# A two-layer token mixer on one NeuronCore: new numbers for the build-time order of its instructions, and the squares of two token tiles put behind the first tile's scaling

## The chip, the cores and the metric

The kernel runs on one core of one Trainium2 chip. The metric is the device time of one launch in microseconds (us). An execution under the profiler also gives a trace: every instruction of TensorE (PE), its weight loads (PEld), VectorE (DVE), ScalarE (ACT), GpSimd (POOL) and SyncE (SP, which issues most transfers), with start and end.

## What is computed

One inference step through two layers, for 128 context tokens and 256 latent tokens of width 1024, three tiles of 128 tokens in all. The context tokens have their own modulation and read only themselves; the latent tokens also read cached keys, values and recurrent states.

```python
def trunk_layer(x, mod, p, lb_f, lb_b, rope, ctx_k, ctx_v, s0_f, s0_b):
    sh1, sc1, g1, sh2, sc2, g2 = jnp.split(mod, 6, axis=-1)
    h = rmsnorm(x, p['norm1_g']) * (1 + sc1) + sh1
    proj = h @ p['w_in']
    q_r, f_f, f_b, i_r, g_r, q_a, k_a, v_a = jnp.split(proj, ...)
    ...
    o_f, s_f = gla_chunked(qr, -jnp.expm1(lf_f), vr, lf_f, s0_f)
    o_b, s_b = gla_chunked(qr[:, ::-1], -jnp.expm1(lf_b)[:, ::-1], vr[:, ::-1], lf_b[:, ::-1], s0_b)
    o_r = rmsnorm(o_f + o_b[:, ::-1], p['hgrn_norm_g']).reshape(B, T, W_R) * jax.nn.silu(g_r)
    ...
    o_a = attend_blocks(qa, k_all, v_all)
    x = x + g1 * (jnp.concatenate([o_r, o_a], axis=-1) @ p['w_out'])
    h2 = rmsnorm(x, p['norm2_g']) * (1 + sc2) + sh2
    x = x + g2 * (jnp.square(jax.nn.relu(h2 @ p['w1'])) @ p['w2'])
    return x, ka, va, s_f, s_b
```

`mod` is `silu(c) @ w_mod + b_mod`, `gla_chunked` a gated linear recurrence run in both directions (4 heads of 128), `attend_blocks` a softmax attention with 8 query and 2 key heads of 64. A last rmsnorm ends both outputs.

## The kernel before

Every large product is made in three passes: a weight is split into a rounded high part (`hi`, a cast on ACT, L413) and the rest (`lo`, a subtraction on DVE, L421), the activations likewise (`Hh`, `Hl`; `mAh`, `mAl`), and TensorE adds hi·Hh, hi·Hl and lo·Hh. These are the **dense** steps: w_in by tokens (L615), by features (L669) and for queries and keys (L639, L640), w_out (L703), w1 (L1218, L1233) and w2 (L1244), 256 to 512 columns a step.

Between them stand TensorE's small groups. In the kernel's words their kinds are "m": modulation products (L457, L468), the levels of the recurrence (L1012, L1026) and the products of attention with V (L927); "t": transposes (L479, L557, L762, L821, L822, L881, L916, L1095, L1148, L1283); "f": scores of attention (L859, L897) and the recurrence's states and outputs (L1101, L1124, L1127, L1128). Several work on a half or a quarter of the array (64 or 32 rows or columns).

No engine's program is written out by hand. Each piece of work is a generator that yields steps `S(engine, duration, function, reads, writes, buffers acquired, buffers released, kind, hold)`. At build time the planner `Sched` (L42 to L148) plays them against a simple clock with estimated durations, and emits, over and over, the step that can go first. Three things weigh in its choice. `start_of` adds `hold` to a small PE step's time when TensorE is in a dense stretch (L100), so that the step lets dense steps pass until others of its sort are ready; between two small groups only `min(hold, SLACK)` counts. `SWITCH` is the cost that the planner believes a change of kind has. And the number given to `spawn` ranks chains when several could go at once. HOLD_M stands at modulation products and their transposes and at L762, HOLD_A in attention, HOLD_Q at the transposes of queries and keys, HOLD_O at the recurrence's states and outputs, HOLD_L at its levels.

At the start, three token tiles `x_92`, `x_93`, `x_94` arrive by DMA. For each, `rms_steps` squares one half on ACT and one on DVE (L533), adds (L539), raises to the power −1/2 on POOL (L541), and `norm_half` scales (L552) and transposes (L557). In the recurrence's output, ACT squares the heads, DVE forms the mean squares (L522), POOL the power (L524), DVE scales with the gate (L1143), TensorE transposes (L1148), and ACT and DVE split the result into `Hh` and `Hl` (L1153) for w_out.

Of the kernel before, what the change touches and what calls it, by code (L numbers as in the profile page):

```python
# [19 lines left out]
SMC = 480  # L20
LAG = HEAD + 1
HOLD_L = 1.0
HOLD_M = 2.0
HOLD_A = 1.0
HOLD_O = 1.0
HOLD_Q = 1.0
BX_T = 0
QN = 3
QG = 2
SLACK = 0.5  # L30
FG_P = 3.0
AP_ACT = ((1, 0),)
HFM = (1,)
# [7 lines left out]
class Sched:  # L41
# [3 lines left out]
    LAT = {"PE": 0.2, "DVE": 0.19, "ACT": 0.13, "POOL": 0.15, "SP": 0.1}  # L45
    OWN = {"PE": 0.0, "DVE": 0.06, "ACT": 0.14, "POOL": 0.1, "SP": 0.0}

    SWITCH = {("d", "m"): 0.11, ("d", "f"): 0.1, ("d", "t"): 0.02, ("m", "d"): 0.2, ("f", "d"): 0.1, ("t", "d"): 0.09,
              ("m", "t"): 0.09, ("m", "f"): 0.05, ("f", "m"): 0.09, ("f", "t"): 0.05, ("t", "m"): 0.09, ("t", "f"): 0.01}
    DMA0, DMA1 = 1.3, 1.8  # L50
    DMAE = 0.7
# [116 lines left out]
def step_kernel(tc, A):  # L168
    nc = tc.nc
    sch = Sched()  # L170
# [34 lines left out]
    x = [sb(f"x{t}", [128, 1024]) for t in range(NT)]  # L205
# [166 lines left out]
    def split_prio():  # L372

        left = sum(1 for k in sch.bound if k[0] == "lo")
        return 0.5 if left <= 1 else 6

    def rcls(u):
        return "raw0" if u in early else "raw"
# [46 lines left out]
    def mod_acc(l, tag):  # L425
        us = mod_units(l, tag)
        acc = {(i, h): ("modacc", l, tag, i, h) for i in range(2) for h in range(2)}
        for u in us:
            for i in range(2):
                for h in range(2):  # L430
                    def f(u=u, i=i, h=h):
                        raw = get(("raw",) + u)[:, h * 512:(h + 1) * 512]
                        o, c = get(acc[i, h]), cT[:, u[3], i:i + 1]
                        if u is us[0]:
                            V.tensor_scalar(out=o, in0=raw, scalar1=c, scalar2=None, op0=ALU.mult)
                        else:
                            V.scalar_tensor_tensor(out=o, in0=raw, scalar=c, in1=o, op0=ALU.mult, op1=ALU.add)  # L437
                    yield S("DVE", c_dve(512, u is us[0], 1), f, r=[("rawk",) + u, "cT"], acq=([("t2", acc[i, h])] + ([("mtok", ("mtok", l, tag))] if (i, h) == (0, 0) else [])) if u is us[0] else [],
                            rel=[("raw",) + u] if (i, h) == (1, 1) else [], w=[("modacck", l, tag, i, h)] if u is us[-1] else [], key=u)

    def mod_chain(l, tag):
# [29 lines left out]
        if tag[0] == "n":  # L471
# [5 lines left out]
            def tr():  # L477
                for s_ in range(ns):
                    PE.transpose(get(nm2)[:, s_ * 128:s_ * 128 + rw], get(ev)[0:rw, s_ * 128:(s_ + 1) * 128], ident[0:rw, 0:rw])  # L479
            yield S("PE", 0.11 * ns, tr, kind="t", hold=HOLD_M if l or tag[:2] != ("n", 0) else 0.0, r=[nm + (1,), "ident"], acq=[("ps", nm2)], rel=[ev], w=[nm + (2,)])  # L480
            jn = J // 2
# [44 lines left out]
    def rms_steps(nm, t, xi, ss):  # L526

        ps = parts(xi, t)
        for n, (c0, c1) in enumerate(ps):
            j = nm + ("j", n)  # L530
            if (xi, n) == (0, 1) or n == 2:

                yield S("DVE", c_dve(c1 - c0, False, 1), lambda: V.scalar_tensor_tensor(out=get(j)[:, 0:c1 - c0], in0=x[t][:, c0:c1], scalar=1.0, in1=x[t][:, c0:c1], op0=ALU.mult, op1=ALU.mult, accum_out=ss[:, n:n + 1]),  # L533
                        r=[("x", xi, t, c0)], acq=[("t2", j)], rel=[j], w=[nm + ("ss", n)])
            else:
                yield S("ACT", c_act(c1 - c0, False, 1), lambda: ACT.activation(out=get(j).bitcast(BF16)[:, 0:c1 - c0], in_=x[t][:, c0:c1], func=AF.Square, accum_out=ss[:, n:n + 1]),
                        r=[("x", xi, t, c0)], acq=[("t2", j)], rel=[j], w=[nm + ("ss", n)])
            if n:
                yield S("DVE", 0.13, lambda: V.tensor_scalar(out=ss[:, 0:1], in0=ss[:, 0:1], scalar1=ss[:, n:n + 1], scalar2=D * EPS if n == 1 else None, op0=ALU.add, **({"op1": ALU.add} if n == 1 else {})),  # L539
                        r=[nm + ("ss", n - 1), nm + ("ss", n)], w=[nm + ("ms",)] if n == len(ps) - 1 else [])  # L540
        yield S("POOL", 0.46, lambda: PO.tensor_tensor(out=ss[:, 0:1], in0=ss[:, 0:1], in1=pw[:, 0:1], op=ALU.pow), r=[nm + ("ms",), "ini"], w=[nm + ("rs",)])  # L541
# [306 lines left out]
    def att_pair(l, t, g):  # L848
# [29 lines left out]
        def tr():  # L878
            for kv in range(2):
                for j in range(3):  # L880
                    PE.transpose(get(pt[kv])[:, j * 128:(j + 1) * 128], get(pp[kv])[:, j * 128:(j + 1) * 128], ident)  # L881
        yield S("PE", 0.66, tr, kind="t", hold=HOLD_A, r=[nm + (3,)], acq=[("ps", pt[0]), ("ps", pt[1])], rel=pp, w=[nm + (4,)])

# [505 lines left out]
    with tc.manual_schedule():  # L1389
        sch.spawn(start_chain(), 0)  # L1390
        sch.spawn(early_reg(), 0)
        sch.spawn(warm_chain("warm", ["ini"], ("h", 0, 0, 0, 0), 21), 99)
        sch.spawn(const_chain(), 4)
        sch.spawn(load_chain(), 5)
        sch.spawn(hi_chain(), split_prio)
        sch.spawn(lo_chain(), split_prio)
        for l in range(L):
            sch.spawn(brow_chain(l), 4)
            for tag in mod_tags(l)[0] + mod_tags(l)[1]:
                if (l, tag) in mod_dve:  # L1400
                    sch.spawn(mod_acc(l, tag), 5.25)
                sch.spawn(mod_chain(l, tag), 0.1 if (l, tag[:2]) == (0, ("n", 0)) else 1 if (l, tag) in mod_dve else 3)
            if l == 0:
                sch.spawn(start_norm(), 0.2)
            for t in range(NT):
                for g in norm_chain(l, 0, t, 2 * l, lambda: Hh, lambda: Hl, [("wo_pe_done", l - 1)] if l else []):
                    sch.spawn(g, 2 + 0.3 * t * 0.6 if l else 1 + 0.1 * t)
            sch.spawn(rope_prep(l), 3)
            sch.spawn(ck_chain(l), 3)
            for t in range(NT):  # L1410
                sch.spawn(qk_chain(l, t), 2.6)
            sch.spawn(attn_region(l), 1)
            for t in range(NT):
                sch.spawn(att_open(l, t), 1)
            for kv in range(2):
                sch.spawn(att_head_ctx(l, kv), 3.0)
            sch.spawn(att_pv(l, 0), 2)
            for t in (1, 2):
                for g in range(4):
                    sch.spawn(att_pair(l, t, g), 3)  # L1420
                sch.spawn(att_pv(l, t), 2)
            for hp in range(2):
                sch.spawn(hg_reg(l, hp), 1)
                for h2 in range(2):
# [88 lines left out]
```

## Time and profile before

| | us |
|---|---|
| median of three runs | 980.83 (980.47 to 981.52) |
| the profiled execution | 980.09 |
| its span, first to last instruction | 978.3 |
| TensorE busy | 967.2 |
| DVE busy | 686.6 |
| ACT busy | 500.1 |

Busy time is the union of an engine's instructions. Matmuls overlap in the trace: the next starts before the last one has ended, so what a dense step costs is the distance from one start to the next, not its length. The span is 1.8 us shorter than the execution's own time.

### The profile page before, as it was taken

The page shows a single profiled execution, that of the slowest core. Times are in us where ns is not written, and L with a number is a line of the kernel's source. Part 1 is how long each engine was busy: PE and PEld are TensorE (multiplying, and loading weights), DVE is VectorE, ACT ScalarE, POOL GpSimd, SP SyncE. Part 2 cuts the span into 40 slices and gives each one's busy share as a digit, 9 for nine tenths or more (in the row PEclk, how much of TensorE's full clock was granted, in tenths as well). Part 3 has the DMA queues.
Part 4 walks back from the last instruction along what each step waited for, and adds up shares of the span by engine and source line. Part 5 has one row for each costly group of instructions (what it writes and reads, how often), then busy time and mean ns, then how long its engine had stood idle before and what let it go on. Part 6 is the DMA issues. An engine that isn't in the chain of part 4 may idle for free.

```text
span 978.3 us, 17379 instructions
## 1 busy us (share of the span) xinstructions
PE 967.2 (99%) x6936; PEld 836.8 (86%) x6936; DVE 686.6 (70%) x1187; ACT 500.1 (51%) x913; POOL 34.5 (4%) x37
## 2 busy tenths in 40 slices
PE   8999999999999999999999999999999999999997
PEld 5796788889989889889888988888899999999896
DVE  4687687777787989989585969977765444444436
ACT  4566656555543444444454676645664444444332
POOL 0020000100000000000001000001100000000000
PEclk9999999999999999999999999999999999999999
DMA  9967676343677887877534322334246444454511
GB/s 313 306 180 237 220 244 178 88 151 94 193 242 241 255 255 234 245 249 236 174 102 126 102 65 88 114 94 141 86 140 209 147 124 144 145 152 148 193 44 64
DMA packets 140656, 165.39 MB, mean 169 GB/s; under 512 B 5872, under 2 KB 105616, under 8 KB 140064
## 3 DMA queue, kind: packets, MB, share of 16 engines
q1 hardware_dynamic: 140144, 163.50, 54.2%
q8 instruction: 54, 0.88, 0.4%
q10 hardware_dynamic: 432, 0.79, 0.2%
q14 instruction: 26, 0.21, 0.1%
HBM read 161.35 MB, written 2.92 MB: 168 GB/s over the span
## 4 chain that ended last, share of the span: by engine, by line
PE 93%; DMA 3%; DVE 1%; issue 1%; ACT 1%; POOL 1%; SPq 0%; POOLq 0%; ACTq 0%; DVEq 0%
PE bank L1244 26%; PE bank L1218 26%; PE bank L669 11%; PE bank L615 7%; PE bank L703 6%; PE bank L639 3%; PE bank L468 2%; PE bank L1026 2%; PE bank L640 1%; PE bank L927 1%; PE bank L881 1%; PE bank L859 1%; DMA eB<-w_mod_d 1%; PE bank L557 1%; DMA raw<-w_in_d 1%
## 5 line engine op out<-in xcount | busy, mean ns | idle before, releaser
L421 DVE TENSOR_TENSOR lo<-raw,hi 128x1024 fp32r<-128x1024 f32 (+1 forms) x149 | 176.9, 1198 | 51.7 <-ACT hi L413 49.9
L413 ACT CAST hi<-raw 128x1024 fp32r<-128x1024 f32 (+1 forms) x149 | 152.8, 1033 | 103.5 <-DMA raw<-w_d 45.3
L437 DVE SCALAR_TENSOR_TENSOR t<-raw,cT,t 128x512 f32<-128x512 f32 x196 | 135.2, 747 | 8.2 <-DMA raw<-w_mod_d 8.0
L1218 PE MATMUL bank<-mA,hi 128*128 128x384 f32 (+1 forms) x336 | 111.5, 332 | 0.0
L1218 PE MATMUL bank<-mA,lo 128*128 128x384 f32 (+1 forms) x336 | 111.1, 331 | 0.0
L1218 PE MATMUL bank<-mB,hi 128*128 128x384 f32 (+1 forms) x336 | 110.9, 330 | 0.0
L1206 DVE TENSOR_TENSOR mB<-t,mA 128x384 fp32r<-128x384 f32 x64 | 35.7, 558 | 102.9 <-ACT mA L1205 102.9
L1203 ACT ACTIVATE t<-bank 128x384 f32<-128x384 f32 x64 | 31.4, 491 | 140.4 <-PE bank L1218 140.4
L1244 PE MATMUL bank<-lo,mA 128*128 128x512 f32 (+1 forms) x255 | 99.3, 389 | 0.0
L1244 PE MATMUL bank<-hi,mB 128*128 128x512 f32 (+1 forms) x255 | 99.2, 389 | 0.0
L1244 PE MATMUL bank<-hi,mA 128*128 128x512 f32 (+1 forms) x255 | 99.0, 388 | 0.0
L1218 PE MATMUL bank<-mA,wts 128*128 128x384 f32 (+1 forms) x352 | 89.4, 327 | 0.0
L1244 PE MATMUL bank<-wts,mA 128*128 128x512 f32 (+1 forms) x268 | 87.8, 389 | 0.0
L413 ACT CAST wts<-raw 128x1024 fp32r<-128x1024 f32 x44 | 46.1, 1050 | 46.4 <-DMA raw<-w_d 23.4
L421 DVE TENSOR_TENSOR wts<-raw,wts 128x1024 fp32r<-128x1024 f32 x44 | 53.7, 1223 | 21.6 <-ACT wts L413 21.3
L669 PE MATMUL bank<-Hh,hi 128*128 128x384 f32 x192 | 67.8, 353 | 0.0
L1218 PEld LDWEIGHTS bank<-mA,hi 128*128 128x128 f32 x336 | 63.2, 188 | 1.9 <-issue 0.4
L669 PE MATMUL bank<-Hh,lo 128*128 128x384 f32 x192 | 64.5, 336 | 0.0
L1218 PEld LDWEIGHTS bank<-mB,hi 128*128 128x128 f32 x336 | 63.2, 188 | 1.4
L669 PE MATMUL bank<-Hl,hi 128*128 128x384 f32 x192 | 64.4, 335 | 0.0
L1218 PEld LDWEIGHTS bank<-mA,wts 128*128 128x128 f32 x352 | 62.6, 188 | 1.7 <-issue 0.9
L1218 PEld LDWEIGHTS bank<-mA,lo 128*128 128x128 f32 x336 | 63.2, 188 | 0.0
(272 smaller groups left out, 1951.1 us busy)
## 6 DMA issues: line engine op xcount, KB each, us to landing
raw<-w_d SPq DMA_DIRECT2D x128, 512.0 KB, 4.2
raw<-w_mod_d SPq DMA_DIRECT2D x80, 512.0 KB, 3.7
raw<-w_in_d SPq DMA_DIRECT2D x40, 512.0 KB, 5.2
raw<-w_in_d SPq DMA_DIRECT2D x16, 384.0 KB, 5.3
G<-grow SPq DMA_DIRECT2D x4, 1024.0 KB, 6.8
raw<-w_out_d SPq DMA_DIRECT2D x16, 256.0 KB, 4.5
raw<-w_out_d SPq DMA_DIRECT2D x8, 512.0 KB
eB<-w_mod_d SPq DMA_DIRECT2D x12, 256.0 KB, 5.4
```

The lines of the kernel that those rows point to most:

```text
L413: yield S("ACT", c_act(n), lambda u=u, n=n: ACT.copy(out=get(("hi",) + u)[:, 0:n], in_=get(("raw",) + u)[:, 0:n]), r=[("rawk",) + u] + aft ...
L421: yield S("DVE", c_dve(n), lambda u=u, n=n: V.tensor_tensor(out=get(("lo",) + u)[:, 0:n], in0=get(("raw",) + u)[:, 0:n], in1=get(("hi",) + ...
L437: V.scalar_tensor_tensor(out=o, in0=raw, scalar=c, in1=o, op0=ALU.mult, op1=ALU.add)
L468: PE.matmul(get(nm)[32 * j:32 * j + m, 0:N], cT[:, k, 0:m], raw[:, o:o + N], start=k == 0, stop=k == 7, tile_position=(0, 32 * j))
L615: PE.matmul(ps, a, b, start=(first and k == 0 and i == 0), stop=(last and k == kk - 1 and i == 2))
L639: PE.matmul(get(aq), a, b[:, 0:512], start=st and i == 0, stop=sp and i == 2)
L669: PE.matmul(ps, a, b, start=(k == 0 and i == 0), stop=(k == 7 and i == 2))
L703: PE.matmul(ps, a, b, start=j == 0 and i == 0, stop=j == 7 and i == 2)
L1203: yield S("ACT", c_act(384, True), lambda: ACT.activation(out=get(r_)[:, 0:384], in_=get(z)[:, 0:384], func=AF.Relu), r=[z], acq=[("t2", r ...
L1206: yield S("DVE", c_dve(384), lambda: V.tensor_tensor(out=get(u)[1], in0=get(t_)[:, 0:384], in1=get(u)[0].bitcast(F32), op=ALU.subtract), r ...
L1218: PE.matmul(get(z)[:, cs], a, b, start=(k == 0 and i == 0), stop=(k == 7 and i == 2))
L1244: PE.matmul(get(bank)[:, c0 % 512:c0 % 512 + c1 - c0], a, b, start=(f == f0 and i == 0), stop=(f == fl and i == 2))
```

## The change

Five of the holds, `SLACK` and three entries of `SWITCH` get other values; the ranks get names, and of those three get other values: the recurrence's levels (3.5 to 3.0), its states (3 to 3.5) and the activation of the MLP (2 to 3.0). In `rms_steps` the squares on DVE of tiles 1 and 2 in the first norm (`xi == 0 and t`) now also depend on the second half of tile 0's scaling. No step is added or taken away by hand; one more warm-up matmul (L315) results.

```diff
-HOLD_M = 2.0
-HOLD_A = 1.0
-HOLD_O = 1.0
-HOLD_Q = 1.0
+HOLD_M = 3.0
+HOLD_A = 3.0
+HOLD_O = 1.5
+HOLD_Q = 2.0
...
-SLACK = 0.5
+P_LV = 3.0
+P_ST = 3.5
+P_ACTV = 3.0
...
+SLACK = 0.3
...
-    SWITCH = {("d", "m"): 0.11, ("d", "f"): 0.1, ("d", "t"): 0.02, ("m", "d"): 0.2, ("f", "d"): 0.1, ("t", "d"): 0.09,
+    SWITCH = {("d", "m"): 0.11, ("d", "f"): 0.1, ("d", "t"): 0.02, ("m", "d"): 0.25, ("f", "d"): 0.2, ("t", "d"): 0.12,
...
-                        r=[("x", xi, t, c0)], acq=[("t2", j)], rel=[j], w=[nm + ("ss", n)])
+                        r=[("x", xi, t, c0)] + ([("nrm", 0, 0, 0, "xn", 1)] if xi == 0 and t else []), acq=[("t2", j)], rel=[j], w=[nm + ("ss", n)])
...
-                sch.spawn(hg_levels(l, hp), 3.5)
+                sch.spawn(hg_levels(l, hp), P_LV)
...
-                    sch.spawn(hg_state(l, 2 * hp + h2), 3)
+                    sch.spawn(hg_state(l, 2 * hp + h2), P_ST)
...
-            sch.spawn(mlp_act(l), 2)
+            sch.spawn(mlp_act(l), P_ACTV)
```

Where the change shows in the order: in the changed file the lines behind the constants stand 13 higher (L533 is L546 there). Numbers behind names tell buffers apart.

DVE at the start, before: squares (L533), sums (L539) and scalings (L552) of the three tiles `x_92` to `x_94`.

```order
L533 SCALAR_TENSOR_TENSOR t_1_108,sm<-x_92 128x512
L539 TENSOR_SCALAR sm<-sm 128x1
L533 SCALAR_TENSOR_TENSOR t_3_110,sm<-x_93 128x512
L552 TENSOR_SCALAR t_4_111<-x_92,sm 128x512
L552 TENSOR_SCALAR t_5_112<-x_92,sm 128x512
```

The same place after the change (squares L546, sums L552, scalings L565):

```order
L546 SCALAR_TENSOR_TENSOR t_1_108,sm<-x_92 128x512
L552 TENSOR_SCALAR sm<-sm 128x1
L565 TENSOR_SCALAR t_3_110<-x_92,sm 128x512
L565 TENSOR_SCALAR t_4_111<-x_92,sm 128x512
L546 SCALAR_TENSOR_TENSOR t_5_112,sm<-x_93 128x512
L546 SCALAR_TENSOR_TENSOR t_7_114,sm<-x_94 128x512
```

Both scalings of `x_92` moved ahead of the squares of `x_93` and `x_94`.

DVE at the end of layer 1's recurrence, before: mean squares (L522), the scaling of two heads of a tile (L1143), their low parts (L1153) and splits of weights (L421) between them.

```order
L1153 TENSOR_TENSOR Hl<-bank_68,Hh 128x2x128
L522 TENSOR_SCALAR sm<-sm 128x2
L421 TENSOR_TENSOR Hl<-raw_115,Hh 128x1024
L1143 SCALAR_TENSOR_TENSOR t_3_110<-bank_63,sm,tok_4628 128x128 x2
L421 TENSOR_TENSOR mA_6273<-raw_117,mA_6273 128x1024
L421 TENSOR_TENSOR lo_124<-raw_118,hi_120 128x1024
L1153 TENSOR_TENSOR Hl<-bank_63,Hh 128x2x128
L522 TENSOR_SCALAR sm<-sm 128x2
L421 TENSOR_TENSOR lo_125<-raw_116,hi_121 128x1024
L1143 SCALAR_TENSOR_TENSOR t_0_107<-bank_68,sm,tok_4628 128x128 x2
```

The same place after (L535, L1156, L1166 and L434 are those four lines):

```order
L434 TENSOR_TENSOR mA_6280<-raw_115,mA_6280 128x1024
L535 TENSOR_SCALAR sm<-sm 128x2
L1156 SCALAR_TENSOR_TENSOR t_7_114<-bank_64,sm,tok_4629 128x128 x2
L535 TENSOR_SCALAR sm<-sm 128x2
L434 TENSOR_TENSOR lo_124<-raw_116,hi_120 128x1024
L1156 SCALAR_TENSOR_TENSOR t_3_110<-bank_65,sm,tok_4629 128x128 x2
L434 TENSOR_TENSOR lo_125<-raw_117,hi_121 128x1024
L1166 TENSOR_TENSOR Hl<-bank_64,Hh 128x2x128
```

The first tile's scaling (`t_7_114`) now follows its mean square with no split between, and the first low part stands behind the second tile's scaling and both splits.

TensorE at the same place after (L1161 transposes scaled heads, L716 is w_out, L1137 to L1141 the outputs):

```order
L1161 MATMUL bank_64<-cst,t_7_114 128x128 x2
L716 MATMUL bank_63<-mA_6280,Hh 128x512
L716 MATMUL bank_63<-mA_6280,Hl 128x512
...
L1137 MATMUL bank_65<-tok_4629,hg_4834 128x128
L1140 MATMUL bank_65<-hg_4834 128x128
L1141 MATMUL bank_65<-S_103,hg_4834 128x128
...
L1161 MATMUL bank_64<-cst,t_3_110 128x128 x2
L716 MATMUL bank_66<-hi_120,Hh 128x512
L716 MATMUL bank_66<-hi_120,Hl 128x512
```

Before, 25 rows of w_out, the six outputs and the transposes of the next tile lay between the first tile's transposes and the step that reads `hi_120` with `Hl`; now four rows of w_out do, beside those outputs and transposes.

TensorE in layer 1, before: products with V (L927) and two groups of level products of the recurrence (L1026), each between dense steps by features (L669).

```order
L669 MATMUL bank_67<-Hh,lo_123 128x384
L927 MATMUL bank_68<-hg_4839,vS_102 64x512 x2
L927 MATMUL bank_68<-hg_4839,vS_100 64x512 x2
L927 MATMUL bank_68<-hg_4839,vS_101 64x512 x2
L669 MATMUL bank_67<-Hh,hi_119 128x384
...
L669 MATMUL bank_64<-Hh,lo_124 128x384
L1026 MATMUL bank_66<-hg_4838,ones 32x32 x24
L669 MATMUL bank_64<-Hh,hi_120 128x384
...
L1026 MATMUL bank_61<-hg_4838 32x32 x24
```

The same work after (L940 the products with V, L1039 the levels, L682 the dense steps):

```order
L682 MATMUL bank_67<-Hh,lo_125 128x384
L1039 MATMUL bank_61<-hg_4833,ones 32x32 x24
L940 MATMUL bank_68<-hg_4834,vS_102 64x512 x2
L940 MATMUL bank_68<-hg_4834,vS_100 64x512 x2
L940 MATMUL bank_68<-hg_4834,vS_101 64x512 x2
L1039 MATMUL bank_62<-hg_4833 32x32 x24
L682 MATMUL bank_67<-Hh,hi_121 128x384
```

Three excursions from the dense steps have become one.

More of the change, by code (lines that the diff above doesn't have):

```diff
@@ L29 @@
 QG = 2
-SLACK = 0.5
+P_EV = 5.062
+P_MA = 5.25
+P_LV = 3.0
+P_ST = 3.5
+P_HO = 3.6
+P_QK = 2.6
+P_AP = 3.0
+P_AC = 3.0
+P_IG = 1.0
+P_SG = 1.5
+P_ACTV = 3.0
+P_SP = 6.0
+LEFT = 1
+SLACK = 0.3
 FG_P = 3.0
@@ L374, in split_prio @@
         left = sum(1 for k in sch.bound if k[0] == "lo")
-        return 0.5 if left <= 1 else 6
+        return 0.5 if left <= LEFT else P_SP
     def rcls(u):
@@ L1400, in step_kernel @@
                 if (l, tag) in mod_dve:
-                    sch.spawn(mod_acc(l, tag), 5.25)
+                    sch.spawn(mod_acc(l, tag), P_MA)
                 sch.spawn(mod_chain(l, tag), 0.1 if (l, tag[:2]) == (0, ("n", 0)) else 1 if (l, tag) in mod_dve else 3)
@@ L1410, in step_kernel @@
             for t in range(NT):
-                sch.spawn(qk_chain(l, t), 2.6)
+                sch.spawn(qk_chain(l, t), P_QK)
             sch.spawn(attn_region(l), 1)
@@ L1415, in step_kernel @@
             for kv in range(2):
-                sch.spawn(att_head_ctx(l, kv), 3.0)
+                sch.spawn(att_head_ctx(l, kv), P_AC)
             sch.spawn(att_pv(l, 0), 2)
@@ L1419, in step_kernel @@
                 for g in range(4):
-                    sch.spawn(att_pair(l, t, g), 3)
+                    sch.spawn(att_pair(l, t, g), P_AP)
                 sch.spawn(att_pv(l, t), 2)
@@ L1424, in step_kernel @@
                 for h2 in range(2):
-                    sch.spawn(hg_ev(l, hp, h2), 5.062)
-                    sch.spawn(hg_sig(l, hp, h2), 1.5)
-                sch.spawn(hg_levels(l, hp), 3.5)
+                    sch.spawn(hg_ev(l, hp, h2), P_EV)
+                    sch.spawn(hg_sig(l, hp, h2), P_SG)
+                sch.spawn(hg_levels(l, hp), P_LV)
                 for h2 in range(2):
-                    sch.spawn(hg_state(l, 2 * hp + h2), 3)
+                    sch.spawn(hg_state(l, 2 * hp + h2), P_ST)
                 for t in range(NT):
-                    sch.spawn(hg_out(l, hp, t), 3.6)
+                    sch.spawn(hg_out(l, hp, t), P_HO)
                 sch.spawn(hg_fin(l, hp), 3)
             for t in range(NT):
-                sch.spawn(ig_chain(l, t), 1.0)
+                sch.spawn(ig_chain(l, t), P_IG)
                 sch.spawn(xupd_chain(l, "wo", t, 0), 0.03 + 0.3 * t * 0.6)
```

## The prediction

> **What bounds the kernel now.** I read the page first, then TensorE's waits, then its timeline row by row.
>
> ```profile
> span 978.3 us, 17379 instructions
> PE 967.2 (99%) x6936; PEld 836.8 (86%) x6936; DVE 686.6 (70%) x1187; ACT 500.1 (51%) x913; POOL 34.5 (4%) x37
> PEclk9999999999999999999999999999999999999999
> PE 93%; DMA 3%; DVE 1%; issue 1%; ACT 1%; POOL 1%; SPq 0%; POOLq 0%; ACTq 0%; DVEq 0%
> PE bank L315 <- DVE sel L264: 2.1, 1, 2.1
> PE bank L479 <- ACT t L475: 0.9, 2, 0.5
> PE bank L557 <- DVE t L552: 0.6, 1, 0.6
> PE bank L1148 <- DVE t L1143: 0.5, 1, 0.5
> ```
>
> TensorE is busy for 99% of the span, the clock granted is full in every slice, and the chain that ends last is 93% TensorE. Its waits, with the longest ones shown, come to some 4 us, half of that ahead of its first matmul. The next engine, DVE, is busy for 70%. So no other engine can pay unless it makes TensorE wait or stops doing so, and the time is TensorE's own stream: dense matmuls, whose number does not change, small groups put between them, what it costs to leave and re-enter the dense stream, and a few waits.
>
> **The change, part by part.** Counted from the two orders of instructions, TensorE does the same matmuls but for one more warm-up matmul (L315). What moves is their grouping: excursions out of the dense stream fall from 105 to 91, changes of kind from 262 to 233. The question is what an excursion costs beside its own matmuls. Columns of the timeline: start, time from start to end, engine, line, result and operands, shape, number.
>
> ```profile
> 80.58 0.34 PE L669 MATMUL bank<-Hh,lo 128*128 128x384 f32 x1
> 80.75 0.81 PE L881 MATMUL bank<-cst,tok 128*128 128x128 f32 x6
> 81.58 0.34 PE L669 MATMUL bank<-Hl,hi 128*128 128x384 f32 x1
> ...
> 581.20 0.34 PE L669 MATMUL bank<-Hh,lo 128*128 128x384 f32 x1
> 581.38 1.47 PE L881 MATMUL bank<-cst,tok 128*128 128x128 f32 x12
> 582.86 0.34 PE L669 MATMUL bank<-Hl,hi 128*128 128x384 f32 x1
> ```
>
> *Transposes.* Between the two L669 rows of each piece lie the transposes and one more dense step (its row is left out). A 384-column step takes 0.17 from start to start (80.58 to 80.75), so six transposes cost 81.58 − 80.58 less two dense steps of 0.17 = 0.66, and twelve 582.86 − 581.20 − 0.34 = 1.32: 0.11 each, both times, and nothing for the excursion itself. **Fusing two groups of transposes saves nothing.**
>
> ```profile
> 157.69 0.39 PE L615 MATMUL bank<-hi,Hl 128*128 128x512 f32 x1
> 157.92 0.39 PE L615 MATMUL bank<-lo,Hh 128*128 128x512 f32 x1
> 158.23 0.63 PE L1026 MATMUL bank<-hg 128*32 128x32 f32 x48
> 158.79 0.50 PE L615 MATMUL bank<-hi,Hh 128*128 128x512 f32 x1
> 159.13 0.40 PE L615 MATMUL bank<-hi,Hl 128*128 128x512 f32 x1
> ...
> 620.12 0.39 PE L615 MATMUL bank<-lo,Hh 128*128 128x512 f32 x1
> 620.44 1.15 PE L1026 MATMUL bank<-hg 128*32 128x32 f32 x96
> 621.51 0.50 PE L615 MATMUL bank<-hi,Hh 128*128 128x512 f32 x1
> 621.85 0.39 PE L615 MATMUL bank<-hi,Hl 128*128 128x512 f32 x1
> ```
>
> *Groups on a quarter or half of the array* (level products L1026, and with them mod products L468, scores L859, products with V L927). A dense 512-column step takes 0.23 (157.69 to 157.92). The group starts 0.31 after the last dense one (157.92 to 158.23): 0.08 of entry. The first dense step behind it takes 0.34 (158.79 to 159.13): 0.11 of return. One excursion of 48 costs 159.13 − 157.92 − 0.46 = 0.75, one of 96 costs 621.85 − 620.12 − 0.46 = 1.27, so two fused save 0.23. I count, behind the first 45 us, 4 entries and 9 returns to dense fewer (returns fall more because some of these groups now lead into transposes): 4 × 0.08 + 9 × 0.11 = **−1.3**. The ends: 12 excursions fewer at the whole 0.19 give −2.3; if a return is merely deferred through the transposes, 4 × 0.19 = −0.8.
>
> The Trainium skill, in "TensorEngine Tiling (Array Packing)", section Key Properties, says "Mode switching requires drain: Changing tiling mode (not just tile) drains the TensorE". That speaks against the change, since transposes and dense steps share one mode. By the orders changes of shape fall only from 146 to 140; by the rule that is six drains, at an estimate of 0.19 each −1.1. The transposes above, without a constant of their own, agree with it.
>
> *The start.*
>
> ```profile
> 6.22 0.69 DVE L533 SCALAR_TENSOR_TENSOR t<-x 128x512 f32<-128x512 f32 x1 [0.25 <-DMA x<-x_sample_d]
> 6.83 0.88 DVE L552 TENSOR_SCALAR t<-x,sm 128x512 f32<-128x512 f32 x2
> 6.04 0.55 POOL L541 TENSOR_TENSOR sm<-sm,pw 128x1 f32<-128x1 f32 x1 [5.60 <-DVE sm L539]
> 24.78 0.83 ACT L413 CAST hi<-raw 128x768 fp32r<-128x768 f32 x1 [4.74 <-DMA raw<-w_in_d]
> 25.84 0.33 PE L479 MATMUL bank<-cst,t 128*128 128x128 f32 x1 [0.51 <-ACT t L475]
> 33.36 0.33 PE L479 MATMUL bank<-cst,t 128*128 128x128 f32 x1 [0.39 <-ACT t L475]
> ```
>
> Tile 0's scaling (6.83) waits for tile 1's square (6.22 + 0.69 = 6.91), though POOL had its factor at 6.59; the new dependency puts it some 0.2 earlier. The squares of tiles 1 and 2, of 0.69 each, come behind it, and tile 1's scaling about 1 us later. None of it reaches the end: at 24.78 ACT's cast waited for a DMA, and TensorE at 25.84 is behind that same transfer. SP's order, which issues it, is the same there. If this cover were gone, tile 1's delay would cost its 1 us. Behind that gate the new order fuses two groups of mod products (one entry and return, 0.19) and puts a dense step over the wait at 33.36 (0.39), and leaves one dense step of about 0.35 on the late side: −0.19 − 0.39 + 0.35, and the odd warm-up matmul lies ahead of the gate; **−0.3**, within ±0.5.
>
> *The last part of layer 1's recurrence.*
>
> ```profile
> 673.10 0.44 PE L1148 MATMUL bank<-cst,t 128*128 128x128 f32 x2
> 678.10 0.44 PE L1148 MATMUL bank<-cst,t 128*128 128x128 f32 x2 [0.47 <-DVE t L1143]
> 681.36 0.39 PE L703 MATMUL bank<-hi,Hl 128*128 128x512 f32 x1
> 670.80 1.60 POOL L524 TENSOR_TENSOR sm<-sm,pw 128x2 f32<-128x2 f32 x1 [25.34 <-DVE sm L522]
> 675.87 1.53 POOL L524 TENSOR_TENSOR sm<-sm,pw 128x2 f32<-128x2 f32 x1 [3.47 <-DVE sm L522]
> 678.58 0.70 POOL L524 TENSOR_TENSOR sm<-sm,pw 128x2 f32<-128x2 f32 x1 [1.18 <-DVE sm L522]
> 675.63 1.22 DVE L421 TENSOR_TENSOR lo<-raw,hi 128x1024 fp32r<-128x1024 f32 x1
> 677.43 0.61 DVE L1143 SCALAR_TENSOR_TENSOR t<-bank,sm,tok 128x128 f32<-128x128 f32 x2 [0.59 <-POOL sm L524]
> ```
>
> POOL's power takes 0.70 alone and 1.5 to 1.6 when a split of 1.22 runs on DVE beside it; the scaled heads (L1143) and the transposes (L1148) come behind. Three such transposes waited 0.2, 0.26 and 0.64 here by the gaps in their rows, **1.1 in all**. In the new order the scaling of the first tile stands directly behind its mean square, with no split between, and all three transposes stand at least 0.7 us of TensorE work behind what they need: −1.1. But w_out's first step that reads the low part of the first tile's heads (L703 `hi,Hl`) came 8.3 us behind their transposes (673.10 to 681.36), and now it stands one dense step behind the second tile's transposes; on DVE one split (1.22, `lo_125` in the order of the section on the change) stands between the second tile's scaling and the low part that it reads (`Hl<-bank_64`). Scaled heads finish 0.7 ahead of those transposes, so the split ends at 0.5 behind their start; 0.4 for the difference itself and 0.2 to be seen make 1.1, against about 0.6 until that step (two transposes 0.22, one dense step 0.34): a **new wait of 0.5**. Sum **−0.6**. Ends: −1.1 without it; another split or a power of 1.6 in the way, +1.0.
>
> *Attention.* With scores held for three dense steps' time rather than one, score groups, transposes and products with V of a tile stand closer together, so the softmax between them has less cover. Five places have under 1 us of slack by the orders. I take one miss of 0.3 among them: **+0.3**, ends 0 (all covered, as now) and +1.2 (one split of 1.22 ahead). The last twentieth of the program, with the final norm, is in the same order: nothing. ACT and POOL keep the number of their instructions, and DVE's splits are the same 149.
>
> **Sum:** −1.3 − 0.3 − 0.6 + 0.3 = −1.9. The profiled run took 980.09 (span 978.3, 1.8 around it), so 978.2 by it; it lies 0.74 below the median of the three runs, 980.83, so **978.9** on the median's scale.
>
> **Rivals.**
> - *A, every excursion pays.* If every change of kind costs, transposes included, what a group on a part of the array pays by the rows (0.08 in, 0.11 out, and up to 0.1 more of drain in its last matmuls), the 14 excursions fewer at 0.29 are −4: 976.8. The cheaper return of larger groups speaks for it; the transposes at a flat 0.11 against it.
> - *B, given back.* The holds move excursions later, and what consumed them early then waits; each of the five tight places in attention in both layers loses 0.15 and the recurrence's waits return: −1.9 + 1.5 = −0.4, 980.4. For it: TensorE waits for nearly nothing now because its orders were loose. Against: DVE is idle for 30% of the span.
> - *C, slower: w_out waits for the mixed heads of layer 1.* Low parts come behind DVE's splits, in order. With a power at 1.6 rather than 0.7 and two splits rather than one ahead of the low part, the wait named above is 0.5 + 0.9 + 1.22 = 2.6 rather than 0.5, and layer 0 has the same chain: −1.9 + 2.1 + 2.6 = +2.8, 983.6. It decides from the point where the chain behind the transposes takes more than the 0.6 us of cover. For it: the 1.53 power at 675.87; against: in the new order the splits stand behind, not ahead of, the first scaling.
> - *It doesn't do what it says:* the square's new dependency has no effect on TensorE, as costed above; that is part of the forecast.
>
> **How the numbers follow.** The forecast, 977.9 to 979.9 (its largest unknown, the fusing, runs from −2.3 to −0.8), has 0.52; A 0.14; B 0.24; C 0.10. A measurement of this kernel can tell about 0.2%, 1.96 us, from no change, that is 978.87 and 982.79. The forecast sits on the lower one, so half of it counts as faster: 0.26 + 0.14 = 0.40; no change 0.26 + 0.24 = 0.50; slower 0.10. The range leaves out C and the far half of A: 976.8 to 981.5.
>
> **What would show it.** Right: the three waits of L1148 gone, transposes still at 0.11 each whatever the size of their group, two level groups with the product with V between them costing one entry and one return, a wait of about 0.5 at w_out's first low part, TensorE's first dense step behind the DMA at the same time within 0.1. Wrong: the dense step behind transposes becoming longer or shorter (A), new rows in TensorE's waits from DVE on scores or transposes of attention (B), a wait over 1 us at w_out (C). What I can't see in the trace of before is how DVE's queue stands at each of these places: that would be what makes it wrong.

## The result, and the profile after

| | before | after |
|---|---|---|
| median, us | 980.74 (980.47 to 981.52, 4 runs) | 986.83 (985.82 to 987.49, 4 runs) |
| profiled execution, us | 980.09 | 986.21 |
| its span, us | 978.3 | 984.4 |

The changed kernel takes 1.0054 times as long, with an interval of 1.0042 to 1.0066: it is 6.1 us slower, where 1.9 us faster was forecast. The page of the changed kernel, its first lines:

```profile
span 984.4 us, 17384 instructions
PE 968.5 (98%) x6935; PEld 837.9 (85%) x6937; DVE 685.7 (70%) x1187; ACT 499.4 (51%) x913; POOL 41.3 (4%) x37
PEclk9999999999999999999999999999999999999999
```

The profiled execution of e1 below (1188.15, at a granted clock of 0.75) was a slow one and gives no row by place; all other times here are of fast ones. The clock is the same and the engines do the same work, but for one figure: POOL is busy for 41.3 us rather than 34.5 with the same 37 instructions. TensorE's waits after (total, number, longest), without those in the first 10 us and those under 0.4:

```profile
PE bank L835 <- DVE t L820: 1.1, 1, 1.1
PE bank L834 <- DVE t L828: 1.0, 2, 0.8
PE bank L481 <- DMA raw<-w_mod_d: 0.9, 1, 0.9
PE bank L1161 <- DVE t L1156: 0.8, 1, 0.8
PE bank L716 <- DVE t L1156: 0.7, 1, 0.7
PE bank L1137 <- ACT t L1123: 0.6, 1, 0.6
```

Only one of these pairs stood in the list of before, the transposes of scaled heads (L1161 is L1148 there: 0.5, at 678.10 in layer 1); after, its wait stands in layer 0. To see where they fall, I weighed each TensorE instruction of the two traces with the same standard time for its shape and noted when each kernel had done the same amount. The table shows, for stretches named by the time in the kernel before, how much later (or earlier, negative) the other kernel left a stretch than it entered it; the experiments below have their rows in it too. Each row is from one execution, so that a few tenths of a microsecond say little.

| us, against before | 0–36 start | 36–72 queries, keys | 72–192 attention, w_in | 192–210 recurrence outputs | 210–269 w_out, w1 | 269–534 MLP | 534–659 layer 1 attention | 659–701 layer 1 outputs | rest | all |
|---|---|---|---|---|---|---|---|---|---|---|
| after | 0.9 | **2.7** | 0.9 | **3.1** | −0.2 | 0.4 | −1.6 | −0.6 | 0.4 | 6.2 |
| e2 holds | 0.7 | −0.8 | −0.4 | 0.2 | 4.1 | 0.5 | −1.5 | −1.5 | 0.5 | 1.8 |
| e3 after, quiet | 0.7 | −0.1 | 1.3 | 1.1 | 3.5 | 0.1 | −0.3 | 3.9 | 0.0 | 10.3 |
| e4 before, quiet | 0.3 | −0.1 | 1.0 | 0.0 | 3.6 | 0.0 | 0.0 | −1.2 | 0.0 | 3.5 |
| e5 after, heads | −0.1 | 0.1 | 0.6 | 1.1 | −0.2 | 0.4 | −0.3 | 4.1 | 0.1 | 5.8 |
| e6 before, heads | 0.3 | −0.1 | 0.8 | 0.0 | −0.2 | 0.4 | 0.0 | −1.1 | 0.0 | 0.0 |
| e7 after, old switch | 0.0 | −0.8 | −0.6 | 1.4 | −0.2 | 0.4 | −1.4 | 3.5 | 0.0 | 2.4 |
| e8 after, old holds | 0.9 | 1.3 | 2.2 | 0.0 | −0.2 | 0.4 | 0.4 | −0.3 | 0.0 | 4.7 |
| e9 holds, layer 1 | 1.3 | −0.1 | 0.1 | 0.0 | −0.2 | 0.3 | −1.4 | −1.5 | 0.5 | −1.1 |
| e10 holds, split | 0.5 | −0.8 | 0.5 | 0.0 | −0.3 | 0.5 | −1.4 | −1.5 | 0.5 | −2.1 |
| e11 after, no power | 1.0 | 0.6 | 0.4 | 1.7 | −0.3 | 0.4 | −1.6 | −0.7 | 0.4 | 2.1 |
| e12 repaired | 1.3 | −0.8 | 1.6 | 0.0 | −0.3 | 0.1 | −1.4 | 5.1 | 0.0 | 5.7 |

So two places of layer 0 lose 5.8 us, and layer 1 gains 2.2. The waits in the list explain 2.1 of the 2.7 (L835, L834) and 2.1 of the 3.1 (L1161, L716, L1137); what is left is in no wait that the profile lists. The first place, in the changed kernel: DVE and POOL at the mean squares of queries and keys (L535 mean squares, L434 splits, L537 the power, L798 the scaling), and the transpose of a key that waits (L835).

```profile
59.58 0.38 DVE L535 TENSOR_SCALAR sm<-sm 128x8 f32<-128x8 f32 x4
59.86 2.36 DVE L434 TENSOR_TENSOR lo<-raw,hi 128x1024 fp32r<-128x1024 f32 x2
64.07 0.29 DVE L798 TENSOR_TENSOR t<-bank,sm 128x128 f32<-128x128 f32 x1 [1.85 <-POOL sm L537]
59.89 6.06 POOL L537 TENSOR_TENSOR sm<-sm,pw 128x10 f32<-128x10 f32 x2 [1.95 <-DVE sm L535]
65.81 0.33 PE L835 MATMUL bank<-cst,t 128*128 128x128 f32 x1 [1.09 <-DVE t L820]
```

POOL's power begins 0.03 after two splits have begun on DVE. Two such powers take 6.06, where before two took 3.89:

```profile
54.10 3.89 POOL L524 TENSOR_TENSOR sm<-sm,pw 128x10 f32<-128x10 f32 x2 [44.69 <-DVE sm L522]
```

The second of the pair in the changed kernel has no split beside it and takes its 1.95; the first takes 4.1, and it ends 1.8 after the splits' end at 62.22, which is nearly a whole power. **The power did not run slowly beside the splits: it stood until they had ended.** DVE then had nothing to do for 1.85, and TensorE waited for the key. The second place, layer 0's recurrence outputs, DVE and POOL in the changed kernel:

```profile
203.19 0.17 DVE L535 TENSOR_SCALAR sm<-sm 128x2 f32<-128x2 f32 x1
203.27 1.22 DVE L434 TENSOR_TENSOR lo<-raw,hi 128x1024 fp32r<-128x1024 f32 x1
205.08 0.61 DVE L1156 SCALAR_TENSOR_TENSOR t<-bank,sm,tok 128x128 f32<-128x128 f32 x2 [0.59 <-POOL sm L537]
203.44 1.61 POOL L537 TENSOR_TENSOR sm<-sm,pw 128x2 f32<-128x2 f32 x1 [24.86 <-DVE sm L535]
205.84 1.60 POOL L537 TENSOR_TENSOR sm<-sm,pw 128x2 f32<-128x2 f32 x1 [0.80 <-DVE sm L535]
208.24 1.60 POOL L537 TENSOR_TENSOR sm<-sm,pw 128x2 f32<-128x2 f32 x1 [0.80 <-DVE sm L535]
```

Three times a split stands between mean square and scaling, three times the power takes 1.60 and ends 0.56 after the split (203.27 + 1.22 = 204.49; 203.44 + 1.61 = 205.05). Before, no split stood there, and the same three powers took 0.70 each (1.41 for two):

```profile
193.18 1.41 POOL L524 TENSOR_TENSOR sm<-sm,pw 128x2 f32<-128x2 f32 x2 [17.04 <-DVE sm L522]
195.39 0.70 POOL L524 TENSOR_TENSOR sm<-sm,pw 128x2 f32<-128x2 f32 x1 [0.80 <-DVE sm L522]
```

And there the outputs all lay ahead of w_out (the last at 193.61, w_out from 195.80); now they lie among its steps, and the transposes wait:

```profile
206.71 0.38 PE L1161 MATMUL bank<-cst,t 128*128 128x128 f32 x2
207.88 0.59 PE L1161 MATMUL bank<-cst,t 128*128 128x128 f32 x2 [0.80 <-DVE t L1156]
```

### The profile page after: what moved, and what is told of

Read it like the earlier page. It is cut to its first block, busy times and chain, and to the rows that moved or that the text cites. A ratio compares the mean times of both kernels' runs of the same rounds, so it can differ in the third digit from the quotient of the medians.

```text
span 984.4 us, 17384 instructions
## 1 busy us (share of the span) xinstructions
PE 968.5 (98%) x6935; PEld 837.9 (85%) x6937; DVE 685.7 (70%) x1187; ACT 499.4 (51%) x913; POOL 41.3 (4%) x37
## 4 chain that ended last, share of the span: by engine, by line
PE 88%; DVE 2%; issue 1%; POOL 1%; DMA 1%; ACT 0%; POOLq 0%; DVEq 0%; ACTq 0%
PE bank L1257 26%; PE bank L1231 26%; PE bank L682 9%; PE bank L628 7%; PE bank L716 6%; PE bank L1039 2%; PE bank L652 1%; PE bank L1246 1%; PE bank L894 1%; PE bank L481 1%; PE bank L940 1%; PE bank L872 1%; PE bank L570 1%; PE bank L470 1%; PE bank L1114 1%
## 5 line engine op out<-in xcount | busy, mean ns | idle before, releaser
L434 DVE TENSOR_TENSOR lo<-raw,hi 128x1024 fp32r<-128x1024 f32 (+1 forms) x149 | 176.6, 1196 | 43.8 <-ACT hi L426 42.2
L434 DVE TENSOR_TENSOR wts<-raw,wts 128x1024 fp32r<-128x1024 f32 x44 | 53.5, 1221 | 22.0 <-ACT wts L426 22.0
L682 PE MATMUL bank<-Hh,hi 128*128 128x384 f32 x192 | 66.7, 347 | 0.0
L682 PE MATMUL bank<-Hh,lo 128*128 128x384 f32 x192 | 64.4, 335 | 0.0
L682 PE MATMUL bank<-Hl,hi 128*128 128x384 f32 x192 | 64.3, 335 | 0.0
```

The costliest lines, as they stand in the source:

```text
L434: yield S("DVE", c_dve(n), lambda u=u, n=n: V.tensor_tensor(out=get(("lo",) + u)[:, 0:n], in0=get(("raw",) + u)[:, 0:n], in1=get(("hi",) + ...
L682: PE.matmul(ps, a, b, start=(k == 0 and i == 0), stop=(k == 7 and i == 2))
```

## Experiments

Theory 1 is this: the splits hold POOL's power, and the scalings behind it are late. Theory 2: TensorE's groups were moved too close to their producers, whatever stands on DVE. Ratios are against the kernel before, run on the same chip; its median there was 980.79 to 981.96, so times in microseconds shift by up to one between experiments. The edits are shortened: constants that stand on lines of their own are put on one.

**e1: SWITCH and SLACK alone.**

```diff
-SLACK = 0.5
+SLACK = 0.3
-    ("m", "d"): 0.2, ("f", "d"): 0.1, ("t", "d"): 0.09,
+    ("m", "d"): 0.25, ("f", "d"): 0.2, ("t", "d"): 0.12,
```

> The kernel before with SWITCH and SLACK alone changed. Theory 1 (a POOL power does not start while a DVE split of 128x1024 runs): in this order DVE has a split directly behind the mean squares of two of layer 0's query/key tiles, and none at the recurrence outputs of either layer, so the transposes of queries and keys at 60 to 70 us wait 1.5 to 2.5 us more, the waits at 670 to 680 go (-1.1): 981 to 982.5. Theory 2 (the transposes only stand too close to their producers, splits or not): the group of recurrence outputs is later here too, some 3 us at 195 to 215: 983 to 985.

982.76, ratio 1.0014 (1.0004 to 1.0023). The time lies between the two ranges, 0.26 above theory 1's and 0.24 below theory 2's. Against the kernel before on the same chip (981.39) it is 1.4 more. Counted from the 980.83 of before, theory 1 had 0.2 to 1.7 and theory 2 2.2 to 4.2, so the difference speaks for theory 1; in which place it was lost is not known.

**e2: the holds alone** (four of the five change, not five as said above; HOLD_L stays at 1.0).

```diff
-HOLD_M, HOLD_A, HOLD_O, HOLD_Q = 2.0, 1.0, 1.0, 1.0
+HOLD_M, HOLD_A, HOLD_O, HOLD_Q = 3.0, 3.0, 1.5, 2.0
```

> The kernel before with the four holds alone changed. Theory 1: no split behind the mean squares of queries and keys, splits behind three of the mean squares of the recurrence outputs but only one ahead of their scaling: nothing at 60 to 70, 1 to 2 us of waits at 195 to 215: 981.5 to 983. Theory 2: what the changed kernel lost at 60 to 70 (2.3 us) comes from the longer hold of these transposes and shows here: 984 or more.

981.58, ratio 0.9997 (0.9987 to 1.0007). The time is in theory 1's range, by luck. Nothing is lost at queries and keys (−0.8), so the hold is not the cause there. But I had the place of the other loss wrong: the outputs lost 0.2, and 4.1 fell behind them, at the start of w1:

```profile
242.00 0.39 PE L1218 MATMUL bank<-mA,lo 128*128 128x256 f32 x1 [1.95 <-DVE lo L421]
```

A low part of w1 came late. My reading, not tried apart, is that the recurrence's work, pushed into w_out's time, took the time of DVE that its split had before. Behind the wait the clock granted to TensorE fell, which costs as well (PEclk is the figure behind POOL's):

```profile
242.00:243.20 1.20, 1.20 (x10) 1.20 (x11) 1.20 (x3) 0.27 (x1) 0.00 (x0) 1.00 0.33 41
243.20:246.60 3.40, 3.40 (x19) 3.40 (x18) 1.97 (x4) 0.00 (x0) 0.00 (x0) 0.50 0.83 283
```

At half the clock, 3.4 us do the work of 1.7. That and the wait of 1.95 are 3.65 of the 4.1; a wait of 0.7 at 231.62 is the rest, within what the method can tell. The gains are in layer 1: 3.0 us.

**e3 and e4: the changed kernel, and the kernel before, with a quiet rule:** the planner gives DVE no split between a mean square and the end of its power (lines of e3 and e5 stand 5 higher than in the changed kernel).

```diff
+        if eng == "DVE" and key is not None and key != "ms":
+            s = max(s, self.hush)
...
+            if key == "ms":
+                self.hush = e + self.LAT["DVE"] + hold
```

On DVE, `key` is set on splits, on the sums of modulation products and on mean squares, so the rule puts off those sums too; `hold` of a mean square is the planner's time for its power.

> The changed kernel, with one rule more in the planner: no split goes to DVE between a mean square and the end of its power on POOL. Theory 1: powers of 2 columns take 0.70 and those of 10 columns 1.95 at the query/key tiles of layer 0 and at the recurrence outputs, and the waits there (2.3 and 3.2 us) shrink by at least two thirds: 981.5 to 983.5. Theory 2: the waits stay, 985.5 to 987.

> The kernel before with the same rule. Theory 1: the waits at 670 to 680 (1.1 us) shrink by half or more, the rest as before: 979.8 to 980.6. Theory 2: 980.5 to 981.

e3 took 989.32, ratio 1.0082 (1.0066 to 1.0097), and e4 983.56, ratio 1.0023 (1.0011 to 1.0035): both times missed, above the ranges of both theories. By place, theory 1 holds at these two places: in e3 queries and keys go from 2.7 to −0.1 and the outputs from 3.1 to 1.1, in e4 layer 1's outputs gain 1.2. But the rule also kept splits away from the powers of the token norms, and w1 then waited for them (a loss of 3.5 in e3 and 3.6 in e4, with 3.4 us at a clock of 0.50 behind the wait in both); and e3's order loses 3.9 at layer 1's outputs, as e5's does below. TensorE in e3:

```profile
244.79 0.39 PE L1236 MATMUL bank<-mA,lo 128*128 128x256 f32 x1 [2.22 <-DVE lo L439]
```

A split beside a power costs the power 0.9, and there it was the right place for it all the same: the power's end was worth less than the split's, as e5 confirms.

**e5 and e6: the same rule at the recurrence outputs and at queries and keys only.** Against e3:

```diff
-   w=[nm + ("ms",)] if n == len(ps) - 1 else [], key="ms" if n == len(ps) - 1 else None, hold=0.46)
+   w=[nm + ("ms",)] if n == len(ps) - 1 else [])
```

> The changed kernel with the quiet rule at the recurrence outputs and at queries and keys only, not at the norms of tokens, whose splits w1 needs at 240. Theory 1: as in e3 the waits at 60 to 70 and 195 to 215 shrink by two thirds or more, and the 2.4 us wait of w1 on a low part at 242 is not there: 981.5 to 983.5. Theory 2 (what e3 lost at 242 comes from the recurrence's splits that were put off, not from the norms): the wait at 242 stays, 985 to 988.

> The kernel before with that narrower rule. Theory 1: the waits at 673 and 678 go, nothing else moves: 0.6 to 1.0 below before. Theory 2: the wait at 240 stays as in e4, 1.5 to 2.5 above before.

e5: 985.74, ratio 1.0050 (1.0035 to 1.0065). e6: 980.62, ratio 1.0000 (0.9991 to 1.0010). The wait at 242 is gone, so it had come from the norms. e5's time lies in theory 2's range all the same, and e6's in neither. POOL in e5 at the two places:

```profile
59.34 3.88 POOL L542 TENSOR_TENSOR sm<-sm,pw 128x10 f32<-128x10 f32 x2 [3.09 <-DVE sm L540]
199.55 0.70 POOL L542 TENSOR_TENSOR sm<-sm,pw 128x2 f32<-128x2 f32 x1 [24.86 <-DVE sm L540]
201.04 0.70 POOL L542 TENSOR_TENSOR sm<-sm,pw 128x2 f32<-128x2 f32 x1 [0.80 <-DVE sm L540]
```

The powers take what they take alone, and both places recover as forecast or nearly (2.7 to 0.1; 3.1 to 1.1). Yet the time did not follow: the splits put off make another order, and layer 1's outputs lose 4.1 in it (waits for a scaled head, an ACT copy and low parts of w_out). e6 keeps its gain of 1.1 there and gives 0.8 back in 72 to 192, without a wait that stands out.

**e7 and e8: the changed kernel with the old SWITCH and SLACK, and with the old holds.**

```diff
-SLACK = 0.3
+SLACK = 0.5
-    ("m", "d"): 0.25, ("f", "d"): 0.2, ("t", "d"): 0.12,
+    ("m", "d"): 0.2, ("f", "d"): 0.1, ("t", "d"): 0.09,
```

That is e7; e8 is:

```diff
-HOLD_M, HOLD_A, HOLD_O, HOLD_Q = 3.0, 3.0, 1.5, 2.0
+HOLD_M, HOLD_A, HOLD_O, HOLD_Q = 2.0, 1.0, 1.0, 1.0
```

> The changed kernel with SWITCH and SLACK of before; holds, ranks and the square's dependency as changed. If the loss at 60 to 70 comes from SWITCH and SLACK and that at 195 to 215 from the holds: no split behind the mean squares of queries and keys, under 0.3 us lost there; 1.5 to 3.2 us still lost at 195 to 215; 982.5 to 984.5. If the query/key loss comes from the hold of their transposes, it stays at 2 us or more.

> The changed kernel with the holds of before; SWITCH, SLACK, ranks and the square's dependency as changed. If the loss at 195 to 215 comes from the holds: the recurrence outputs of the second head pair stand ahead of w_out's steps again, under 0.5 us lost there, 1.5 to 2.5 still lost at 60 to 70, and the layer 1 waits at 670 to 680 go too: 981.5 to 983. Otherwise 984 or more.

e7: 982.37, ratio 1.0021 (1.0011 to 1.0030). e8: 984.77, ratio 1.0044 (1.0029 to 1.0059). The two losses part as forecast: without the new SWITCH and SLACK queries and keys gain 0.8 and the outputs still lose 1.4; without the holds the outputs lose nothing and queries and keys 1.3, though the 1.4 and the 1.3 are a little under what was expected. Both times missed, e7's by a little, and e8's lies where the other reading was put (984 or more), since each has a loss that the changed kernel doesn't have: 3.5 in e7 at layer 1's outputs, 2.2 in e8 in layer 0's attention.

**e9 and e10: the kernel before with the holds by layer.**

```diff
-HOLD_M, HOLD_A, HOLD_O, HOLD_Q = 2.0, 1.0, 1.0, 1.0
+HOLD_A, HOLD_O = (1.0, 3.0), (1.0, 1.5)
+HOLD_M, HOLD_Q = (2.0, 3.0), (1.0, 2.0)
-    hold=HOLD_A
+    hold=HOLD_A[l]
```

That is e9 (every hold of the four is taken by layer, `[l]`, the first of the pair in layer 0); e10 has `HOLD_M, HOLD_Q = (3.0, 3.0), (2.0, 2.0)`.

> The kernel before with the four longer holds in layer 1 only. If the holds' loss sits in layer 0 alone (the recurrence outputs pushed into w_out, and w1's wait on a low part at 240 behind them) and their gain in layer 1's attention and recurrence (2 us in e2 by the trace), this keeps layer 0 as before and gives 978.5 to 979.5. If the gain there came from the shift in time that layer 0 caused, 980.5 to 981.

> As e9, and the longer holds of modulation products and of query/key transposes in layer 0 too; those of attention and of the recurrence's outputs in layer 1 only. With e2's gain at 60 to 80 (0.5 to 0.8) on top of e9: 977.8 to 979. If that gain needs the hold of attention too: as e9.

e9: 978.90, ratio 0.9967 (0.9955 to 0.9979). e10: 978.80, ratio 0.9967 (0.9958 to 0.9977). Both beat both kernels, by 3.1 us against the kernel before in the medians and by 1.1 and 2.1 in the table's single executions. Layer 1 keeps its gains, layer 0's outputs stay as before, and w1 does not wait. e10 from e9 can't be told apart by their times. The page of e10, and all waits of 0.4 and more in it:

```profile
span 976.2 us, 17381 instructions
PE 963.5 (99%) x6934; PEld 836.6 (86%) x6936; DVE 686.1 (70%) x1187; ACT 499.5 (51%) x913; POOL 32.8 (3%) x37
```

```profile
PE bank L557 <- DVE t L552: 2.5, 3, 1.6
PE bank L315 <- DVE sel L264: 2.1, 1, 2.1
PE bank L479 <- ACT t L475: 1.0, 2, 0.6
```

POOL is at 32.8, below the 34.5 of before: fewer splits stand beside powers.

**e11: the changed kernel without POOL's power**, in the same order: DVE multiplies by a constant right behind the mean square, so the norms of queries, keys and recurrence outputs lack their power. Its lines behind the edit stand one higher.

```diff
+            V.tensor_tensor(out=ss, in0=ss, in1=pw[:, 0:n], op=ALU.mult)
-        yield S("POOL", 0.29 + 0.166 * n, lambda: PO.tensor_tensor(out=ss, in0=ss, in1=pw[:, 0:n], op=ALU.pow), ...)
+        yield S("POOL", 0.29 + 0.166 * n, lambda: None, ...)
```

> The changed kernel with the power on POOL left out for queries, keys and recurrence outputs (DVE multiplies the mean squares by a constant in its place, right behind them, so the norms are not those of the reference); TensorE's, ACT's and SP's orders stay as in the changed kernel, and DVE's splits stay where they are. If the loss is POOL's power held by the splits: of the 2.8 us lost at 60 to 70, 2 or more go, of the 3.1 at 195 to 215, 1.2 to 1.8 (a scaling then starts at the split's end rather than 0.6 later), 982.5 to 984. If the splits ahead of the scalings in DVE's own queue are the loss: under 1.5 us go in all, 985.5 or more.

981.88, ratio 1.0005 (0.9996 to 1.0015); queries and keys lose 0.6 rather than 2.7, the outputs 1.7 rather than 3.1, as forecast. The time is 0.6 below the range, still further from the rival's 985.5; by the ratios 4.8 of the 6.1 us are gone, by the table 4.1. DVE there:

```profile
59.74 2.35 DVE L434 TENSOR_TENSOR lo<-raw,hi 128x1024 fp32r<-128x1024 f32 x2
62.01 0.28 DVE L799 TENSOR_TENSOR t<-bank,sm 128x128 f32<-128x128 f32 x1
```

The splits stand where they stood, and the scaling starts as they end (59.74 + 2.35, less the overlap of the rows), where it came 1.85 later. This is the one experiment that leaves every place of TensorE's order alone, so here place and time agree: the power on POOL, held as it was, is 3.5 of the 6.2 us (2.1 and 1.4). It is the hold and not the power's own 0.70 or 1.95: not held, the power begun at 203.44 would have ended at 204.14, ahead of the split's end at 204.49, and the one begun at 59.89 at 61.84, ahead of 62.22, so each would have cost the scaling nothing. e5, where the powers run at their own times and the two places recover as much or more, agrees, but it moves the splits as well. Of the 1.7 that stay at the outputs, 0.65 are the first outputs' wait for an ACT copy, as in the changed kernel, and 0.2 a wait for a scaled head behind a split; the rest is in no wait that the profile lists. So the splits in DVE's own queue account for little.

**e12: the changed kernel with both repairs**, the old SWITCH and SLACK and HOLD_A, HOLD_O by layer; against e10 it has the ranks and the square's dependency besides.

```diff
-HOLD_A = 3.0
-HOLD_O = 1.5
+HOLD_A = (1.0, 3.0)
+HOLD_O = (1.0, 1.5)
-SLACK = 0.3
+SLACK = 0.5
```

> The changed kernel with SWITCH and SLACK of before and with the longer holds of attention and recurrence outputs in layer 1 only; it differs from e10 by the ranks and the square's dependency. If e7's loss of 3.5 us at 670 to 690 comes from the ranks: 982 to 984. If it came from layer 0's order: 978 to 979.5, as e10.

984.73, ratio 1.0032 (1.0019 to 1.0044). Layer 1's outputs lose 5.1 where e10 gains 1.5. DVE, POOL and TensorE at the worst wait:

```profile
682.56 1.22 DVE L434 TENSOR_TENSOR lo<-raw,hi 128x1024 fp32r<-128x1024 f32 x1
682.73 1.60 POOL L537 TENSOR_TENSOR sm<-sm,pw 128x2 f32<-128x2 f32 x1 [0.80 <-DVE sm L535]
685.03 0.44 PE L1161 MATMUL bank<-cst,t 128*128 128x128 f32 x2 [1.96 <-DVE t L1156]
```

The same chain of split, power and scaling, in an order that the ranks bring as far as can be argued: the square's dependency touches the first norm only, but the two were not tried apart. This wait is 1.96 of the 5.1; three shorter ones (0.68, 0.47 and 0.26) are 1.4, and the clock behind the wait, where w_out's steps stand 0.43 apart rather than 0.23, costs some 1.6 again:

```profile
686.10:689.50 3.40, 3.40 (x11) 2.61 (x10) 1.03 (x3) 0.38 (x1) 0.00 (x0) 0.50 0.69 217
```

Under the new SWITCH and SLACK the ranks do no such harm: the changed kernel gains 0.6 there. No setting is good or bad by itself.

## Why the prediction was wrong

- **What bounds the kernel: right.** DVE's and ACT's busy times are as before, the clock is full, and TensorE's waits make up the larger part of what was lost (4.2 of 5.8 us at the two places).
- **Transposes: right.** After, eight of them from 195.17 cost 196.27 − 194.94 − 0.46 = 0.87 between dense steps of 0.23, 0.11 each as before:

```profile
194.94 0.39 PE L716 MATMUL bank<-lo,mAh 128*128 128x512 f32 x1
195.17 1.03 PE L1108 MATMUL bank<-cst,hg 128*128 128x128 f32 x8
195.96 0.48 PE L716 MATMUL bank<-hi,mAh 128*128 128x512 f32 x1
196.27 0.40 PE L716 MATMUL bank<-hi,mAl 128*128 128x512 f32 x1
```

- **Fusing groups on part of the array, −1.3: right in sign.** In layer 1's attention, where TensorE has no listed wait in either kernel, the changed kernel gains 1.6. The longer holds bring it: e2, e9 and e10 gain 1.4 to 1.5 there, and e8, with the old holds, loses 0.4. The −1.3 was meant for the whole program, so its size is not confirmed. A fused excursion of the changed kernel, start to start:

```profile
599.97 0.34 PE L682 MATMUL bank<-Hh,lo 128*128 128x384 f32 x1
600.24 0.63 PE L1039 MATMUL bank<-hg,ones 128*32 128x32 f32 x48
600.80 2.79 PE L940 MATMUL bank<-hg,vS 128*64 128x512 f32 x12
603.53 0.72 PE L1039 MATMUL bank<-hg 128*32 128x32 f32 x48
604.17 0.44 PE L682 MATMUL bank<-Hh,hi 128*128 128x384 f32 x1
604.45 0.34 PE L682 MATMUL bank<-Hl,hi 128*128 128x384 f32 x1
```

One entry (0.27 for a step of 0.17: 0.10) and one return (0.28: 0.11) where three excursions had three of each.

- **The start, −0.3:** it lost 0.9. That is not the change: e2 and e9, whose first 36 us are ordered as before, lost 0.7 and 1.3, and e5 and e7, which have the square's dependency, −0.1 and 0.0. The stretch moves by a microsecond between executions, and the square is worth nothing that shows.
- **Layer 1's outputs, −0.6:** −0.6 measured, but in part by luck. The wait of 0.5 that was to be new at w_out's first low part did not come: that step starts 0.32 behind the one before it, as the step at 196.27 above starts 0.31 behind its own. The waits that went were thus worth some 0.6, not 1.1; one of 0.25 stands at a transpose of this stretch after as well (L1161 at 677.66).

```profile
687.01 0.48 PE L716 MATMUL bank<-hi,Hh 128*128 128x512 f32 x1
687.33 0.40 PE L716 MATMUL bank<-hi,Hl 128*128 128x512 f32 x1
```

- **Attention, +0.3:** layer 0's 72 to 192 lost 0.9, but nearly all of it is one wait for a transfer of modulation weights (0.9). Its cause stays open: waits like it stand in some of these executions and not in others, and e11, in the same order, has one of 0.4 in another place. The miss of 0.3 between softmax and TensorE did not show.
- **The step that failed** is the one that let DVE's splits go at nothing: "ACT and POOL keep the number of their instructions, and DVE's splits are the same 149." Their number was right; where they stand was looked at in layer 1's outputs alone, where the prediction even used POOL's 1.5 to 1.6 beside a split. In the new order of DVE, which was there to be read, splits also stand behind the mean squares of layer 0's query/key tiles (one at the first tile, two at the pair of the others) and of three of its recurrence outputs. At the price that it had in hand, 0.9 for each split beside a power, the two splits behind one pair of query/key tiles are 1.8 and the three behind the outputs 2.7. The two places lost 2.7 and 3.1, of which e11 puts 2.1 and 1.4 down to the held power: the price would have given the sign and about the size, though too much at the outputs.
- **The rivals.** C had the mechanism, a power held by splits, and its sign, 983.6 and a chance of 0.10; but it looked for it at w_out's low parts and left out queries and keys. Its price was low by 3. B (given back, 0.24) had waits come back behind the holds, but in attention and layer 1's recurrence and for less, 980.4. A (every excursion pays) fell: 14 excursions fewer came with no gain of that size.

The Trainium skill states the rule in "SBUF — State Buffer", section "SBUF: two separate sides": the port pair that VectorE and GpSimd share is an exclusive lock, held for a whole instruction, by a DVE operation with two SBUF inputs too. The splits read `raw` and `hi`, both in SBUF, and the powers that began beside them stood until their end; an operation on DVE that reads a PSUM bank did not hold one (before, the scaling at 193.13 of 0.61 beside the power at 193.18, which took its 0.70). The same section of the Trainium skill has the lock both ways, for whichever starts first; that a power holds up a split the one case here does not show (the split at 56.90 below took its 1.22). The prediction would have been better for reading that page of the Trainium skill beside POOL's rows.

## What to carry to other kernels

When an order changes, list for each slow step of a small engine (here POOL's power) what the large engine beside it runs in the new order, at every place where the step occurs and in every layer, and price it with the rows of the old trace. A fix that shortens such a step but moves others' work is judged by the whole time, not by the step: e3 and e5 cured it and remained slower than the kernel before. And a gain and a loss that sit in different layers can be had apart, by giving the setting per layer (e9, e10: 0.9967).

## What I had not expected of the hardware

A power well under way is not held. In the kernel before, DVE starts a split at 56.90, within the second power of the pair at 54.10 (56.03 to 57.99):

```profile
56.90 1.22 DVE L421 TENSOR_TENSOR lo<-raw,hi 128x1024 fp32r<-128x1024 f32 x1
```

The power takes 1.96 and the split 1.22, each as alone: a power 0.87 under way was not held, and the split that came second did not wait either. In the changed kernel one begun only 0.02 ahead of a split, at 54.88 (the split 54.90), took 3.06. In e9 one of 2 columns, begun as little ahead, took its 0.70:

```profile
167.95 0.70 POOL L524 TENSOR_TENSOR sm<-sm,pw 128x2 f32<-128x2 f32 x1 [101.49 <-DVE sm L522]
167.97 1.24 DVE L421 TENSOR_TENSOR lo<-raw,hi 128x1024 fp32r<-128x1024 f32 x1
```

So at a lead of 0.02 both came; what decides there was not measured.

The other surprise is the clock behind a long wait. In the traces of e2, e3, e4 and e12, TensorE waited for 1.95 to 2.4 us in the midst of its stream, and within 1.2 us behind the wait its granted clock was 0.50 for some 3.4 us, which costs nearly as much again as the wait. In e7 a wait of 1.96 (at 683.28) was followed by the full clock, so the wait alone does not decide it, and the cause was not tried apart.
